# Padded queries in the first attention, modulation steps moved, small loads issued earlier

## The chip, the cores and the metric

The kernel runs on one core of a Trainium2 chip. The metric is the device time of one execution in microseconds (us). The engines, each with its own instruction row that runs in order: TensorE (PE; its weight loads are a row of their own, PEld), VectorE (DVE), ScalarE (ACT), GpSimd (POOL) and SyncE (SP). SP, ACT and POOL also issue the DMA transfers.

## The reference, cut to what matters

Two transformer blocks, batch 1, 256 tokens, width 1024. The change touches the first, which has two layers: differential attention with a gated FFN, then a pooling mixer with a gated FFN. Both layers are modulated by vectors made from `c`.

```python
def adaln_params(cond, w_mod, b_mod):
    m = jax.nn.silu(cond) @ w_mod + b_mod
    return jnp.split(m, N_MOD, axis=-1)

def diff_softmax_mix(q, k, v, lam):
    s = jnp.einsum('bqhmd,bkhmd->bhmqk', q * (HEAD_DIM ** -0.5), k).astype(jnp.float32)
    p = jax.nn.softmax(s, axis=-1)
    a = p[:, :, 0] - lam * p[:, :, 1]
    return jnp.einsum('bhqk,bkhe->bqhe', a.astype(v.dtype), v)

def first_block(...):
    for i in range(DEPTH):                      # 2 layers
        sh1, sc1, g1, sh2, sc2, g2 = adaln_params(c[:, None, :], w_mod[i], b_mod[i])
        hx = h * (1 + sc1) + sh1                # and the same for the context in layer 0
        # layer 0: 8 heads, each with two maps m = 0, 1 of 64 columns; 256 queries, 512 keys
        # layer 1: multi-scale pooling
        x = layer_norm(ALPHA * x + g1 * y_lat, ln_g[i, 0], ln_b[i, 0])
        x = layer_norm(ALPHA * x + g2 * swiglu(modulate(x, sh2, sc2), ffn_w_in[i], ffn_w_out[i]), ln_g[i, 1], ln_b[i, 1])
```

## The kernel before, in words

**Products.** Products of weights and activations are made in three passes (`mm3`, L77 to L80): both operands are split in a high and a low part, and high x high, high x low and low x high are added up in PSUM. A weight block (1 MB) is loaded by SP into one of four `raw` buffers (`raw_load`, L51), and `wsplit` (L57) makes `whi` (an ACT cast, L70) and `wlo` (a DVE subtraction, L71), each in two halves.

**Order.** The program is written in the Tile framework. Its scheduler sets the order of instructions of each engine when the program is built, by its own planning; `behind(...)` keeps an instruction from being issued before another. After that each engine runs its row in order. A DMA of SP or ACT signals its end in one of eight places, taken in turn by both engines' loads; a new load waits for the load that had its place before (`DMAHW0` to `DMAHW7` in the order below).

**Loading.** The loop `for q in range(4)` (L621) loads a quarter of the first two modulation vectors' weights (two raws), a quarter of `x` and of the context, and the rows of the attention's weights for it. `mod_quarter` makes the modulation, `modulate` transposes and modulates the inputs (`hf`, L567), `fill` splits the attention's weights, and `products` and `rest` make the projections of group 0. After the loop seven small loads are issued by ACT behind the last `hf`: five into `prow` (norm gains and biases; transposed by PE at L648 to `pcol`), `rope` (the tables of the rotary embedding) and `lamr`.

**Attention.** Four groups of two heads (L755). `rope_T` rotates the keys and then the queries and transposes them (L690); `split_to` splits them in high and low. A block of scores (`scores`, L693) is one head and one half of the queries: for each of the two maps a 128 x 512 score tile in a PSUM bank of its own (`sbank`, two buffers), in three passes, each over the 64 rows of that map (L706). Then two reductions on DVE (L708), two exps on ACT (L710), and the mix of the maps (L713), which is transposed (L717). There are 16 blocks.

**The modulation stream.** `mod_stream` (L198) makes ten further modulation vectors in ten groups of eight steps; a step is a 512 KB load by POOL into one of three `mraw` buffers (L131) and a multiply and add on DVE (L132). Steps are strewn by `mod_step` over attention (2 behind each score block), the first FFN's first product (3 at a time) and its second product (1 behind each of 11 units). A group ends in `acc_col` (L138) or `acc_row` (L145) on PE. The ninth group is `g1_1`, whose last step is the 72nd.

**The second FFN product** (`Ffn.out`, L452): 11 units of 24 products with 512 columns, of which the last two units' 48 are held for `finish`. Those stand `behind(mods["mm"])` (L846), that is, behind the last L145 of `g1_1`.

## Time and profile before

| | |
|---|---|
| median of 3 runs | 1158.36 us (1158.08 to 1160.95) |
| profiled execution | 1157.81 us, its span 1156.0 us |
| PE busy / PEld busy | 98% / 90% of the span |
| DVE / ACT / POOL busy | 72% / 50% / 7% |
| DMA | 229.69 MB, mean 199 GB/s |
| loading and first modulation | 0 to 72 us |
| attention, 16 score blocks | 72 to 210 us |
| first FFN, first product | 250 to 374 us |
| first FFN, second product | 375 to 439 us |

The stages are read from the trace by the first and last instructions of their lines. A busy share is a mean over stages; where one engine is busy all the time, the others' idle time costs nothing there. Busy time of PE counts an overlap of two matmuls once; the duration of one matmul (the second number of a row of the timeline) is longer than the step to the next one's start, since they are pipelined.

### The profile page before, as it was taken

To read this page: it belongs to the slowest core of one execution; us is meant where nothing else is said; L and a number is where in the kernel's file an instruction comes from. 1 tells how busy PE (TensorE), PEld (TensorE's weight loads), DVE (VectorE), ACT (ScalarE), POOL (GpSimd) and SP (SyncE) were. 2 spreads that over 40 slices of the span, in tenths; PEclk is the share of its full clock that TensorE was granted. 3 is DMA by queue.
4 is the path that set the end of the run, shared out by engine and by line. 5 is a ranking of instruction groups with operands and counts; after the bars stand their busy time and mean duration, and the time that the engine had idled before them with its cause. 6 is when DMAs were issued, how large, how long until landed. Compare 5 with 4: busy or idle time off the path is not lost. (4 is left out here: it accounts for less than half of the span.)

```text
span 1156.0 us, 19870 instructions
## 1 busy us (share of the span) xinstructions
PE 1129.1 (98%) x7967; PEld 1035.3 (90%) x7967; DVE 829.0 (72%) x1547; ACT 575.8 (50%) x1017; POOL 83.9 (7%) x154
## 2 busy tenths in 40 slices
PE   8989999999999999999999889999999999999998
PEld 7979988889999877999988779989999989999986
DVE  5677887887887877856654779788788674655541
ACT  5643444576444436654543655455346356545430
POOL 0101110100111111000000020000100000000000
PEclk9999999999999999999999999999999999999999
DMA  9956545648998993867565353660456254664530
GB/s 311 324 174 212 183 155 174 219 146 285 313 317 291 341 353 121 249 217 257 210 222 175 109 180 121 179 200 29 146 160 223 77 178 147 219 199 167 215 113 37
DMA packets 149098, 229.69 MB, mean 199 GB/s; under 512 B 5708, under 2 KB 121051, under 8 KB 149006
## 3 DMA queue, kind: packets, MB, share of 16 engines
q1 hardware_dynamic: 133440, 176.10, 46.6%
q0 software_dynamic: 14672, 50.63, 13.0%
q10 hardware_dynamic: 894, 1.69, 0.5%
q8 instruction: 63, 1.03, 0.4%
q14 instruction: 29, 0.24, 0.1%
HBM read 226.36 MB, written 2.04 MB: 198 GB/s over the span
## 5 line engine op out<-in xcount | busy, mean ns | idle before, releaser
L71 DVE TENSOR_TENSOR wlo<-raw,whi 128x1024 fp32r<-128x1024 f32 (+2 forms) x318 | 372.7, 1193 | 135.2 <-ACT whi L70 133.7
L70 ACT CAST whi<-raw 128x1024 fp32r<-128x1024 f32 (+2 forms) x318 | 316.3, 1028 | 229.6 <-PE mm L80 86.7
L78 PE MATMUL mm<-hTh,whi 128*128 128x256 f32 x1056 | 299.1, 283 | 0.0
L80 PE MATMUL mm<-hTh,wlo 128*128 128x256 f32 x1056 | 298.9, 283 | 0.0
L79 PE MATMUL mm<-hTl,whi 128*128 128x256 f32 x1056 | 298.3, 282 | 0.0
L79 PEld LDWEIGHTS mm<-hTl,whi 128*128 128x128 f32 x1056 | 199.4, 189 | 0.3
L78 PEld LDWEIGHTS mm<-hTh,whi 128*128 128x128 f32 x1056 | 199.3, 189 | 0.3
L80 PEld LDWEIGHTS mm<-hTh,wlo 128*128 128x128 f32 x1056 | 199.3, 189 | 0.1
L78 PE MATMUL mm<-whi,hTh 128*128 128x256 f32 (+4 forms) x592 | 185.5, 314 | 2.3 <-DVE hTh L336 1.8
L80 PE MATMUL mm<-whi,hTl 128*128 128x256 f32 (+4 forms) x592 | 184.8, 313 | 0.4 <-DVE hTl L337 0.4
L79 PE MATMUL mm<-wlo,hTh 128*128 128x256 f32 (+4 forms) x592 | 184.3, 312 | 0.6 <-DVE wlo L71 0.6
L78 PEld LDWEIGHTS mm<-whi,hTh 128*128 128x128 f32 x592 | 112.4, 190 | 9.0 <-DVE hTh L336 2.9
L79 PEld LDWEIGHTS mm<-wlo,hTh 128*128 128x128 f32 x592 | 112.3, 190 | 4.9 <-DVE wlo L71 1.0
L80 PEld LDWEIGHTS mm<-whi,hTl 128*128 128x128 f32 x592 | 111.9, 189 | 5.2 <-DVE hTl L337 1.0
L132 DVE SCALAR_TENSOR_TENSOR acc<-mraw,csil,acc 128x1024 f32<-128x1024 f32 x80 | 102.2, 1280 | 10.0 <-DMA mraw<-in_w_mod_dram 9.6
L78 PE MATMUL mm<-whi,hid 128*128 128x512 f32 x264 | 104.3, 395 | 0.0
L79 PE MATMUL mm<-wlo,hid 128*128 128x512 f32 x264 | 104.2, 395 | 0.0
L80 PE MATMUL mm<-whi,hid 128*128 128x512 f32 x264 | 103.7, 393 | 0.0
L131 POOL DMA_DIRECT2D mraw<-in_w_mod_dram x80 | 42.6, 533 | 367.8 <-DVE acc L132 269.8
L79 PEld LDWEIGHTS mm<-wlo,hid 128*128 128x128 f32 x264 | 49.6, 188 | 11.6 <-issue 1.0
L80 PEld LDWEIGHTS mm<-whi,hid 128*128 128x128 f32 x264 | 49.6, 188 | 11.5 <-issue 0.7
L78 PEld LDWEIGHTS mm<-whi,hid 128*128 128x128 f32 x264 | 49.6, 188 | 11.4 <-issue 0.7
(329 smaller groups left out, 1556.6 us busy)
## 6 DMA issues: line engine op xcount, KB each, us to landing
raw<-in_ffn_w_in_dram SPq DMA_DIRECT2D x44, 1024.0 KB, 7.1
mraw<-in_w_mod_dram POOLq DMA_DIRECT2D x80, 512.0 KB, 5.0
raw<-in_ffn_w_out_dram SPq DMA_DIRECT2D x22, 1024.0 KB, 4.9
raw<-in_w_ffn_in_dram SPq DMA_DIRECT2D x22, 1024.0 KB, 5.2
raw<-in_w_in_dram SPq DMA_DIRECT2D x16, 1024.0 KB, 5.5
raw<-in_w_ffn_out_dram SPq DMA_DIRECT2D x11, 1024.0 KB, 5.0
raw<-in_w_in_dram SPq DMA_DIRECT2D x14, 768.0 KB, 4.4
raw<-in_attn_w_qkv_dram SPq DMA_DIRECT2D x9, 1024.0 KB, 8.4
```

The lines of the kernel that those rows point to most:

```text
L70: se.copy(hv[:, sl], raw[:, sl])
L71: seq["sub"] = ve.tensor_sub(lv[:, sl], raw[:, sl], hv[:, sl].bitcast(F32)).ins
L78: pe.matmul(o, lh, rh, start=first, stop=False, **kw)
L79: pe.matmul(o, lh, rl, start=False, stop=False, **kw)
L80: return pe.matmul(o, ll, rh, start=False, stop=last, **kw).ins
L131: gp.dma_start(raw, wv[:, k, g * 1024:(g + 1) * 1024])
L132: ve.scalar_tensor_tensor(acc, raw, csil[:, k, 0:1], acc, op0=ALU.mult, op1=ALU.add)
```

## The change

Three things are changed.

1. The queries are kept in a tile `QZ` with 128 rows for each map: the map's own 64 rows hold the query, the other 64 hold zeros, written once by POOL. A score matmul then runs over all 128 rows of the keys and gives the same sums. `split_to` is called once for each map's rows. The passes are written map by map instead of in turns.
2. The small loads into `prow`, `rope` and `lamr` are issued at `q == 1` of the loading loop instead of behind it.
3. The steps of the modulation stream: behind a score block 1 instead of 2; 1 behind the last `rope_T` addition of a group and 2 behind its last mix, so 7 per group instead of 8; in the first FFN's second product 2 at units 2, 4, 6 and 8.

```diff
-STEPS_S, STEPS_IN, STEPS_OUT = 2, 3, 1
+STEPS_S, STEPS_IN, STEPS_OUT = 1, 3, 1
...
             for u in range(11):
                 o.unit(u)
                 with behind(seq["sub"]):
-                    mod_step(mod_out)
+                    mod_step(mod_out * (2 if u in (2, 4, 6, 8) else 1))
...
             modulate(q)
+            if q == 1:
+                with behind(seq["mod"]):
+                    prow = cp.tile([128, 128], F32, name="prow")
+                    gp.memset(prow, 0.0)
+                    se.dma_start(prow[32:64], I["ln_g"].rearrange("l w (k c) -> (l w k) c", c=128))
+                    se.dma_start(prow[64:96], I["ln_b"].rearrange("l w (k c) -> (l w k) c", c=128))
+                    se.dma_start(prow[96:104], rows128(I["norm1_g_2"][0]))
+                    se.dma_start(prow[104:112], rows128(I["norm2_g_2"][0]))
+                    se.dma_start(prow[112:113], I["attn_subln_g"])
+                    rope = at.tile([128, 2, 2, 2, 64], F32, name="rope")
+                    se.dma_start(rope, I["k_rope"].rearrange("(t p) v w c -> p t v w c", p=128))
+                    lamr = at.tile([128, 256], F32, tag="aT", name="lamr", bufs=5)
+                    se.dma_start(lamr, I["attn_lambda"].rearrange("a b c -> a (b c)").to_broadcast([128, 256]))
...
-            ve.tensor_add(r12[:, 0, :], r12[:, 0, :], r12[:, 1, :])
+            seq["rope"] = ve.tensor_add(r12[:, 0, :], r12[:, 0, :], r12[:, 1, :]).ins
...
+        QZ = [at.tile([128, 2, 2, 256], F32R, name=f"QZ{i}") for i in range(2)]
+        for a in QZ:
+            for m in range(2):
+                gp.memset(a[(1 - m) * 64:(2 - m) * 64, m].bitcast(F32), 0.0)
...
-            last = ()
-            for i, (q, k) in enumerate(((qh, kh), (qh, kl), (ql, kh))):
-                for m in range(2):
-                    p = slice(m * 64, (m + 1) * 64)
-                    with behind(*last):
-                        last = pe.matmul(Sm[m], q[p, h, tk], k[p, h, :], start=i == 0, stop=i == 2).ins,
+            for m in range(2):
+                for i, (q, k) in enumerate(((QZ[0], kh), (QZ[1], kh), (QZ[0], kl))):
+                    pe.matmul(Sm[m], q[:, m, h, tk], k[:, h, :], start=i == 0, stop=i == 2)
...
-            rope_T(cq.PL, *[lat(a) for a in qhl], 1)
+            qT = rope_T(cq.PL, 1)
+            for m in range(2):
+                p = slice(m * 64, (m + 1) * 64)
+                split_to(*[lat(a[p, m]) for a in QZ], qT[p])
+            with behind(seq["rope"]):
+                mod_step()
...
+            with behind(seq["mix"]):
+                mod_step(2)
             head_out(aTs, vt, g, sm)
```

SP in the loading, before: from the attention's weight rows of the third quarter (`raw`, 128x2x256) to the modulation weights of the fourth (`raw`, 128x8x256) and its `x`. In brackets stands what an instruction waits for.

```order
L526 DMA raw<-in_attn_w_qkv_dram 128x2x256 [waits DMAHW7_49,DVE_49]
L526 DMA raw<-in_attn_w_qkv_dram 128x2x256 [waits DMAHW0_49]
L498 DMA xin<-in_ctx_dram 128x256 [waits DMAHW1_49]
L498 DMA xin<-in_ctx_dram 128x256 [waits DMAHW2_49]
L526 DMA raw<-in_attn_w_qkv_dram 128x2x256 [waits DMAHW3_49]
L54 DMA raw<-in_w_mod_dram 128x8x256 [waits DMAHW4_49,DVE_49]
L54 DMA raw<-in_w_mod_dram 128x8x256 [waits DMAHW5_49,DVE_49]
L495 DMA x<-in_x_dram 128x2x256 [waits DMAHW6_49]
```

SP, the same loads after:

```order
L526 DMA raw<-in_attn_w_qkv_dram 128x2x256 [waits DMAHW0_49,DVE_49]
L526 DMA raw<-in_attn_w_qkv_dram 128x2x256 [waits DMAHW3_49]
L498 DMA xin<-in_ctx_dram 128x256 [waits DMAHW5_49]
L498 DMA xin<-in_ctx_dram 128x256 [waits DMAHW7_49]
L526 DMA raw<-in_attn_w_qkv_dram 128x2x256 [waits DMAHW1_49]
L54 DMA raw<-in_w_mod_dram 128x8x256 [waits DMAHW3_49,DVE_49]
L54 DMA raw<-in_w_mod_dram 128x8x256 [waits DMAHW4_49,DVE_49]
L495 DMA x<-in_x_dram 128x2x256 [waits DMAHW5_49]
```

The loads are the same and in the same order; the places whose earlier loads they wait for are others, because ACT's seven loads now take places in between.

ACT in the same part, before: the `hf` activations of the second quarter, and the casts of the third quarter's modulation weights (`whi`, L70, and `we`, L514) and attention weights (`whi`, L588).

```order
L70 CAST whi<-raw 128x1024 [waits DMAHW4_49,Activation_49]
L567 ACTIVATE hf<-tp,modc 128x256 [waits PE_49]
L567 ACTIVATE hf<-tp,modc 128x256
L70 CAST whi<-raw 128x1024
L514 CAST we<-raw 128x1024 [waits DMAHW5_49,Activation_49]
L514 CAST we<-raw 128x1024 [waits Activation_49]
L588 CAST whi<-raw 128x512 [waits DMAHW7_49]
```

ACT after; L636 to L644 are the seven small loads:

```order
L567 ACTIVATE hf<-tp,modc 128x256 [waits PE_49]
L567 ACTIVATE hf<-tp,modc 128x256
L636 DMA prow<-in_ln_g_dram 32x128 [waits Pool_49]
L637 DMA prow<-in_ln_b_dram 32x128 [waits DMAHW1_49]
L638 DMA prow<-in_norm_g_dram 8x128 [waits DMAHW2_49]
L639 DMA prow<-in_norm_g_dram 8x128
L640 DMA prow<-in_attn_subln_g_dram 1x128 [waits DMAHW6_49]
L642 DMA rope<-in_k_rope_dram 128x2x256 [waits DMAHW0_49]
L644 DMA lamr<-in_attn_lambda_dram 128x256 [waits DMAHW2_49]
L70 CAST whi<-raw 128x1024
L514 CAST we<-raw 128x1024 [waits DMAHW5_49,Activation_49]
L588 CAST whi<-raw 128x512
```

The small loads moved from behind the fourth quarter's last `hf` to the place between the second quarter's `hf` and the second half of the third quarter's first cast.

PE in group 0 of attention, before: part of the second score block (`s<-k,q`, L706) among projections (L78 to L80).

```order
L80 MATMUL mm<-whi,hTl 128x256
L706 MATMUL s<-k_741,q_739 128x512
L78 MATMUL mm<-whi,hTh 128x256
L79 MATMUL mm<-wlo,hTh 128x256
L80 MATMUL mm<-whi,hTl 128x256
L706 MATMUL s<-k_741,q_739 128x512
L706 MATMUL s<-k_742,q_739 128x512 x2
L706 MATMUL s<-k_741,q_740 128x512 x2
L78 MATMUL mm<-whi,hTh 128x256
L79 MATMUL mm<-wlo,hTh 128x256
```

PE after, the first score block of group 0:

```order
L80 MATMUL mm<-whi,hcTl 128x256
L710 MATMUL s<-k_745,QZ_739 128x512
L710 MATMUL s<-k_745,QZ_740 128x512
L710 MATMUL s<-k_746,QZ_739 128x512
L710 MATMUL s<-k_745,QZ_739 128x512
L710 MATMUL s<-k_745,QZ_740 128x512
L710 MATMUL s<-k_746,QZ_739 128x512
L78 MATMUL mm<-whi,hTh 128x256
L79 MATMUL mm<-wlo,hTh 128x256
L80 MATMUL mm<-whi,hTl 128x256
```

A block was issued in pieces between projections; now its six matmuls with `QZ` stand together or in two threes.

DVE at the end of the first FFN's second product, before: L71 are the splits of the weights of units 8, 9 and 10, and, in the last row, of the next weights; L132 are the steps of the modulation, the last one the 72nd.

```order
L71 TENSOR_TENSOR wlo<-raw,whi 128x1024 [waits DMAHW7_49,Activation_49]
L71 TENSOR_TENSOR wlo<-raw,whi 128x1024 [waits Activation_49]
L132 SCALAR_TENSOR_TENSOR acc<-mraw,csil,acc 128x1024 [waits DMASW6_49,DVE_49]
L71 TENSOR_TENSOR wlo<-raw,whi 128x1024 [waits DMAHW0_49,Activation_49]
L71 TENSOR_TENSOR wlo<-raw,whi 128x1024 [waits Activation_49]
L132 SCALAR_TENSOR_TENSOR acc<-mraw,csil,acc 128x1024 [waits DMASW7_49,DVE_49]
L71 TENSOR_TENSOR wlo<-raw,whi 128x1024 [waits DMAHW1_49,Activation_49]
L71 TENSOR_TENSOR wlo<-raw,whi 128x1024 [waits Activation_49]
L132 SCALAR_TENSOR_TENSOR acc<-mraw,csil,acc 128x1024 [waits DMASW0_49,DVE_49]
L132 SCALAR_TENSOR_TENSOR acc<-mraw,csil,acc 128x1024 [waits DMASW1_49,DVE_49]
L132 SCALAR_TENSOR_TENSOR acc<-mraw,csil,acc 128x1024 [waits DMASW2_49,DVE_49]
L71 TENSOR_TENSOR wlo<-raw,whi 128x1024 [waits DMAHW3_49,Activation_49]
```

DVE after, the splits of units 9 and 10 (the first two pairs of L71), the steps behind unit 8 from the third on, and the next weights' split (the last two L71):

```order
L71 TENSOR_TENSOR wlo<-raw,whi 128x1024 [waits DMAHW0_49,Activation_49]
L71 TENSOR_TENSOR wlo<-raw,whi 128x1024 [waits Activation_49]
L132 SCALAR_TENSOR_TENSOR acc<-mraw,csil,acc 128x1024 [waits DMASW4_49,DVE_49]
L132 SCALAR_TENSOR_TENSOR acc<-mraw,csil,acc 128x1024 [waits DMASW5_49,DVE_49]
L132 SCALAR_TENSOR_TENSOR acc<-mraw,csil,acc 128x1024 [waits DMASW6_49,DVE_49]
L71 TENSOR_TENSOR wlo<-raw,whi 128x1024 [waits DMAHW1_49,Activation_49]
L71 TENSOR_TENSOR wlo<-raw,whi 128x1024 [waits Activation_49]
L132 SCALAR_TENSOR_TENSOR acc<-mraw,csil,acc 128x1024 [waits DMASW7_49,DVE_49]
L132 SCALAR_TENSOR_TENSOR acc<-mraw,csil,acc 128x1024 [waits DMASW0_49,DVE_49]
L71 TENSOR_TENSOR wlo<-raw,whi 128x1024 [waits DMAHW3_49,Activation_49]
L132 SCALAR_TENSOR_TENSOR acc<-mraw,csil,acc 128x1024 [waits DMASW1_49,DVE_49]
L71 TENSOR_TENSOR wlo<-raw,whi 128x1024 [waits Activation_49]
```

Behind the split of unit 8 there are nine steps up to the 72nd, where there were five; the 72nd (its row is the next behind those shown) also has two halves of the next weights' splits ahead of it.

## Rows read from the trace of the kernel before

**Rows 1.** Stretches: busy us of PE, PEld, DVE, ACT, POOL; PEclk; DMA share; GB/s.

```profile
10.00:40.00 30.00, 28.89 (x238) 24.68 (x236) 22.72 (x35) 20.69 (x31) 0.00 (x0) 1.00 1.09 348
66.00:70.00 4.00, 4.00 (x23) 4.00 (x24) 4.00 (x9) 1.53 (x2) 0.00 (x0) 0.61 0.01 4
400.00:420.00 20.00, 20.00 (x90) 16.59 (x89) 17.51 (x15) 7.33 (x8) 3.75 (x8) 1.00 1.00 349
676.00:680.00 4.00, 4.00 (x25) 3.42 (x24) 3.75 (x13) 2.20 (x9) 0.00 (x0) 1.00 0.56 124
```

**Rows 2.** Timeline, PE, second score block: start us, us, instruction.

```profile
75.47 0.28 PE L80 MATMUL mm<-whi,hTl 128*128 128x256 f32 x1
75.68 0.50 PE L706 MATMUL s<-k,q 64*128 64x512 f32 x1
76.11 0.39 PE L78 MATMUL mm<-whi,hTh 128*128 128x256 f32 x1
...
76.45 0.28 PE L80 MATMUL mm<-whi,hTl 128*128 128x256 f32 x1
76.66 0.96 PE L706 MATMUL s<-k,q 64*128 64x512 f32 x5
77.55 0.38 PE L78 MATMUL mm<-whi,hTh 128*128 128x256 f32 x1
```

**Rows 3.** Groups of instructions, 72 to 240: busy us, mean ns of one | idle before.

```profile
L706 PE MATMUL s<-k,q 64*128 64x512 f32 x96 | 22.4, 447 | 0.3
```

**Rows 4.** Timeline, PE, second product of the first FFN.

```profile
400.67 0.39 PE L78 MATMUL mm<-whi,hid 128*128 128x512 f32 x1
...
402.48 0.39 PE L80 MATMUL mm<-whi,hid 128*128 128x512 f32 x1
```

**Rows 5.** Groups of instructions, DVE, 72 to 238: split of the queries.

```profile
L674 DVE TENSOR_TENSOR q<-tp,q 128x512 fp32r<-128x512 f32 x4 | 2.8, 692 | 3.5 <-ACT q L673 3.5
```

**Rows 6.** Waits, 50 to 72 us: total, times, longest (DVE, PE).

```profile
DVE pcol L650 <- PE s L648: 4.5, 1, 4.5
DVE r L684 <- DMA rope<-in_k_rope_dram: 1.6, 1, 1.6
...
PE s L648 <- DMA prow<-in_norm_g_dram: 0.7, 1, 0.7
```

**Rows 7.** Timeline, PE, around the first rotated transposes [idle before <-releaser].

```profile
63.12 0.28 PE L80 MATMUL mm<-whi,hcTl 128*128 128x256 f32 x1
65.94 0.65 PE L690 MATMUL tp<-idsel,r 128*128 128x128 f32 x4 [2.55 <-DVE r L687]
```

**Rows 8.** Timeline, ACT's issues: the first and the last of seven.

```profile
53.21 0.32 ACTq L642 DMA_DIRECT2D prow<-in_ln_g_dram  x1
...
55.73 0.48 ACTq L658 DMA_DIRECT2D lamr<-in_attn_lambda_dram  x1
```

**Rows 9.** Timelines, ACT and SP, in the loading.

```profile
31.19 1.05 ACT L70 CAST whi<-raw 128x1024 fp32r<-128x1024 f32 x1
...
28.73 5.42 SPq L54 DMA_DIRECT2D raw<-in_w_mod_dram  x2
```

**Rows 10.** SP's waits; DMA issues (KB each, us to landing), 0 to 72.

```profile
SPq L54 <- DMA prow<-in_ln_g_dram: 8.2, 1, 8.2
...
prow<-in_ln_g_dram ACTq DMA_DIRECT2D x1, 16.0 KB, 2.9
```

**Rows 11.** Timelines, DVE and PE, at the end of group g1_1.

```profile
420.13 1.28 DVE L132 SCALAR_TENSOR_TENSOR acc<-mraw,csil,acc 128x1024 f32<-128x1024 f32 x1 [0.79 <-DMA mraw<-in_w_mod_dram]
424.49 1.28 DVE L132 SCALAR_TENSOR_TENSOR acc<-mraw,csil,acc 128x1024 f32<-128x1024 f32 x1 [3.07 <-DMA mraw<-in_w_mod_dram]
...
425.31 0.39 PE L80 MATMUL mm<-whi,hid 128*128 128x512 f32 x1
425.87 1.96 PE L145 MATMUL s<-acc,ones 128*128 128x512 f32 x4 [0.17 <-issue]
```

**Rows 12.** Timeline, PE, start of the second block.

```profile
675.73 0.30 PE L956 MATMUL tp<-idsel,pr 128*128 128x128 f32 x1 [3.15 <-DMA pr<-in_qk_norm_g_dram]
```

More of the change, by code (lines that the diff above doesn't have):

```diff
@@ L654, in tile_net @@
             N1, N2 = pcol[:, 96:104], pcol[:, 104:112]
-            rope = at.tile([128, 2, 2, 2, 64], F32, name="rope")
-            se.dma_start(rope, I["k_rope"].rearrange("(t p) v w c -> p t v w c", p=128))
-            lamr = at.tile([128, 256], F32, tag="aT", name="lamr", bufs=5)
-            se.dma_start(lamr, I["attn_lambda"].rearrange("a b c -> a (b c)").to_broadcast([128, 256]))
             lsum = at.tile([128, 4], F32, name="lsum")
@@ L760, in tile_net @@
                 cq.products(ALLK)
[L761 removed]
             khl = [at.tile([128, 2, 512], F32R, tag=f"k{i}", name=f"k{i}", bufs=1) for i in range(2)]
             lat = lambda a: a.rearrange("p h (t c) -> p t h c", t=2)
[L764 removed]
+            split_to(*[lat(a[:, :, 256:512]) for a in khl], rope_T(ck.PL, 0))
             split_to(khl[0][:, :, 0:256], khl[1][:, :, 0:256], ck.PC)
[L766 removed]
+            qT = rope_T(cq.PL, 1)
[4 more added lines that the diff above has]
+                mod_step()
             if not g:
@@ L773, in tile_net @@
                 for h in range(2):
-                    aTs[t, h] = scores(*qhl, *khl, h, t, sm[:, 2 * t + h, :])
+                    aTs[t, h] = scores(*khl, h, t, sm[:, 2 * t + h, :])
                     with behind(seq["mix"]):
```

15 lines of the change are left out of this document (3 added, 12 removed).

## The prediction

> **What bounds the kernel now.** I read the share of busy time per engine first, then stretches of the span, then what TensorE (PE) does at the places the diff touches. In the stretches [rows 1] the reader should see that PE is busy 28.89 of 30 us while the first weights load and 20.00 of 20 us near the end of the first FFN, and that the DMA engines are full in both (share 1.09 and 1.00, 348 and 349 GB/s). So time is won only where PE idles, waits, runs at the lower clock or spends long on few products, and what delays PE costs its full length. Three places count: the start up to 72 us, the 16 score blocks (72 to 210 us), and the second product of the first FFN (375 to 439 us). Outside them the order of work is the same apart from a few shifts.
>
> The sum is made against the profiled execution, 1157.8 us; the median of the runs is 1158.4, so 0.6 is added at the end. A measurement of this kernel can tell about 0.3% (3.5 us) from no change.
>
> **Part 1, scores on 128 rows.** Now a block has six 64-row matmuls of 512 columns, in pairs on opposite halves of the rows. The two of a pair run together: 96 of 447 ns would be 42.9 us, and the line's busy time is 22.4 [rows 3]. But a block is mostly split in two, with a projection matmul between, and each turn from 128-row to 64-row work and back costs extra [rows 2]: from the L80 at 75.47 to the L78 at 76.11 are 0.64 us, where the pitch of these 256-column lines is 0.12 (half of the 0.226 below), so a lone score matmul costs 0.52; the other five, 76.45 to 77.55, cost 1.10 - 0.12 = 0.98. Together 1.50 per block; 12 of the 16 blocks are split so, the other four (six matmuls in one piece) take 1.35 by the same reading. After the change a block is six full-row matmuls of 512 columns. Their price stands in the FFN: eight steps from 400.67 to 402.48 [rows 4], 0.226 each, 1.36 per block. Gain: 12 x 0.14, less 4 x 0.01, about 1.7 us.
>
> Against it: the padded query needs its split in two calls per half of the rows, one VectorE (DVE) subtraction more per group (0.69 us [rows 5]), and one ScalarE (ACT) cast more; the order puts fewer projections between the blocks (13 to 16 instead of 21 to 32), and DVE's chain per block (two reductions, reciprocal, mix, one step of the modulation at 1.28) is about as long as PE's spacing then. The trace shows no such spacing; I take 0.25 us of new waiting per group, 1 us in all, between nothing and 4.8 (0.3 per block). **Part 1: -0.7 us, between -1.7 and +3.1.** The four memsets are on GpSimd (POOL) ahead of any use, the fewer DVE steps (7 for 8 per group) beside PE's work: nothing.
>
> The Trainium skill speaks against this part: "TensorE: Matmul & The Clock Gate", Part 3 on packing small matmuls, says that matmuls on different row groups run at the same time, a few ns apart, and that a lone matmul with few rows takes as long as a full one. The pairs of this trace do start together, so the rule holds for them. By it alone a block would cost 3 x 0.226 = 0.68 now and 1.36 after, a loss of 11 us over 16 blocks; the measured 1.50 of a block, turns included, is why I don't sum by it.
>
> **Part 2, small loads moved up.** What they cost now, at 53 to 70 us: ACT issues the seven loads from 53.21 to 56.21 [rows 8]; PE waits 0.7 us for prow; DVE sits 4.5 us behind the transposed prow and 1.6 for the rope table [rows 6], so the rotated keys are late and PE idles 2.55 us before L690 at 65.94 [rows 7]. Behind that idle time PE's granted clock falls to the 1.2 GHz level: its mean in 66 to 70 is 0.61 [rows 1], which is 0.39 x 4 = 1.6 us of work lost. All of it can go: 0.7 + 2.55 + 1.6 = 4.8 us. It is the whole gain only if nothing is late next.
>
> What is late next: the same seven issues, 3.0 us, now stand in ACT's row in the loading, behind the second quarter's `hf`, ahead of the second half of a weight cast that ran at 31.19 [rows 9]; rope and lamr also wait there for earlier loads of their ring place. Behind that cast on ACT are all casts of the third quarter, and PE's products of it. ACT's idle times later in this quarter are waits for these same products and absorb nothing. On SyncE (SP), the ring of eight completion places is shared: seven are taken by ACT's loads, so that SP's context loads and the first modulation weights of the fourth quarter stand behind them. Before, SP issued those at 28.73 [rows 9]. That such a wait is real the trace shows where the loads now lie: SP sat 8.2 us on a weight load until prow landed, and a prow load takes 2.9 us [rows 10]. From 31.2 (ACT's place) + 0.3 + 2.9 = 34.4: up to 5.7 us late on a queue which keeps the DMA engines full. PE has 1.1 us of idle time in these 30. I take the ACT cost, 3.0 us, between 0 (hidden by products of the quarter before) and 5.7; the likely value is nearer the ACT rows than the SP one, since the DMA engines have some us of work queued. A new idle time could halve the clock once more (1.6). **Part 2: -4.8 + 3.0 = -1.8 us, between -4.8 and +2.5.**
>
> **Part 3, modulation steps spread.** Each of the 80 steps is a 512 KB load by POOL and a DVE instruction of 1.28 us. Attention has 28 instead of 32; the second FFN product 15 instead of 11 (two at units 2, 4, 6, 8). The step that ends the group g1_1, the 72nd, is the same one, and it is a gate: PE's last 48 products of the FFN stand behind L145, which needs that step. Before, the gate was just met: the last product ahead of it is at 425.31, L145 at 425.87; DVE had waited 0.79 and 3.07 us for the loads of the last two steps, which ran at 420.13 and 424.49 [rows 11]. There is no slack, so each us the 72nd step is later is a us of PE. By the order, DVE has nine steps after the split of unit 8 where it had five, and two halves of a weight split before the last. Lower bound, DVE alone: 4 x 1.2 (pitch) + 2 x 1.2 - (0.79 + 3.07) = 3.3 us. By bytes: 4 x 512 KB = 2.1 MB more to land before the gate while the DMA engines are full, at 349 GB/s [rows 1] 6.0 us. Upper: about 8, if loads of the next layer's weights come between. I take the bytes, since DVE's last two waits there were for loads. PE may then idle long enough to fall to 1.2 GHz (1.6 us again); it did after 2.55 us [rows 7], but not after 3.15 us before 675.73 [rows 12], where the stretch behind has 1.00 [rows 1], so this stays in the range. Fewer steps in attention give PE nothing back, as DVE there is hidden behind PE. **Part 3: +6.0 us, between 0 and +9.6** (0: the loads come through faster than the full engines suggest, and the steps end before PE is there).
>
> Sum: 1157.8 - 0.7 - 1.8 + 6.0 = 1161.3; with 0.6, 1161.9 us.
>
> **Rivals.**
> A, *faster: the steps are hidden and the start gains whole.* The steps come two at a time from unit 2 on, and 3 loads are in flight, so loads may run further ahead of PE than I think; ACT's issues may lie beside PE's products of the quarter before. 1157.8 - 4.8 - 1.7 + 0.6 = 1151.9. Against it: full DMA engines in both places.
> B, *no change: the gate costs DVE's time only.* 1157.8 - 0.7 - 1.8 + 3.3 + 0.6 = 1159.2. It decides by whether the loads of the last steps land before DVE asks.
> C, *slower, by the start: the small loads stop the big ones.* SP behind ACT's loads, 5.7 us, and the lower clock again: part 2 is +2.5, the total 1157.8 - 0.7 + 2.5 + 6.0 + 0.6 = 1166.2. It decides from some 4.8 us of delay in the third quarter, where the gain is eaten.
> D, *the padding does double work.* If a pair costs one pitch and the turns are paid in both kernels, a block goes from 3 x 0.226 to 6 x 0.226, and 16 blocks lose 11 us: 1157.8 + 11 - 1.8 + 6.0 + 0.6 = 1173.6. The rows for 1.50 per block speak against it. This is the rule of the Trainium skill told above.
>
> **How the numbers follow.** My forecast has 0.40, with an own range of 1159 to 1166; of it 0.12 falls within 0.3%. A has 0.27, B 0.16, C 0.13, D 0.04. Faster: A, 0.27. Same: B and that 0.12, 0.28. Slower: 0.28 + 0.13 + 0.04 = 0.45. The range that leaves out no more than 2 in 10 goes from the middle of A to the upper part of C: 1152 to 1168.
>
> **What would show it.** Part 1: score blocks of six matmuls 0.23 apart with no turns, and 1.3 to 1.4 us per block; waits for DVE's reductions or exps beside them tell the price against it. Part 2: no idle time of 2.55 before the first rope transpose and no 0.61 behind it, but the weight cast of the third quarter at 34 instead of 31, and SP's loads for the fourth later than 28.7. First scores earlier than before show a net gain. Part 3: PE idle by 4 to 8 us before L145 of g1_1 with DVE or the mraw loads as releaser. If PE passes that gate with under a microsecond of waiting, my forecast is wrong and A is right; if the start is later than before, C is.

## The result, and the profile after

The changed kernel takes 1174.3 us (median of 4 runs, 1170.6 to 1175.1) where the kernel before takes 1159.2: the ratio is 1.0133, with a 95% interval of 1.0116 to 1.015. It is 15 us slower; 3.5 had been forecast, and the time lies above the stated range of 1152 to 1168. The profiled execution is 1175.1 us, the slowest of its four and 17.3 more than that of before, so the shares below add up to 17.3 and not to 15.

Where the time went can be read by lining the two traces up by work: each matmul of PE is taken at its columns divided by 2.4 GHz, added up over PE's row, and for a point of the trace before I looked when the changed kernel had done as much. The table is worked out so from the traces (us later than the profiled execution of before; negative is earlier); the columns are times of the trace before. 55 lies in the loading, 72 at the first scores, 250 behind attention and its output product, 374 behind the first FFN's first product, 425 just ahead of the gate, 445 behind it. The kernels from e1 on are the experiments below.

```
kernel           55     72    250    374    425    445   1150
after         +11.9   +6.5   +4.6   +5.5   +6.0  +17.1  +17.3
e1_loads_old   +0.8   +1.0   -1.3   -0.5    0.0  +11.7  +12.0
e2_steps_old  +12.3   +7.0   +8.0   +8.1   +8.1   +7.7   +7.6
e3_qz_only      0.0   -0.2   +2.6   +2.6   +2.6   +2.5   +1.7
e4_loads_only  +7.4   +1.6   +1.4   +1.4   +1.4   +2.4   +2.3
e7_no_gate     +9.4   +4.1   +2.2   +3.0   +3.2   +8.4  +10.3
e9_steps_in   +12.7   +7.4   +5.4  +12.2  +12.2  +13.0  +13.5
e10_loads_sp   +1.4   -3.8   -5.6   -4.8   -4.2   +5.8   +5.8
e12_best       +0.1   -5.1   -2.3   -2.3   -2.3   -1.5    0.0
e13_before_sp  +0.1   -5.5   -5.8   -5.8   -5.8   -5.9   -6.1
e16_act_dummy  +3.9   -1.9   -2.1   -2.1   -2.1   -2.4   -2.7
e20_rope2       0.0   -4.7   -5.1   -5.1   -5.1   -5.4   -4.6
```

So the loading lost 11.9 us and got 5.4 of them back by the start of the scores (the idle time and the lower clock of [rows 7] and [rows 1] are gone); attention gained 1.9, of which 1.4 were lost again up to 425; the gate cost 11.1.

**The loading.** Stretches of the changed kernel; columns as in [rows 1]:
```profile
28.00:34.00 6.00, 6.00 (x52) 5.76 (x52) 3.52 (x7) 2.97 (x5) 0.00 (x0) 1.00 0.74 222
34.00:40.00 6.00, 3.62 (x30) 2.38 (x29) 4.56 (x5) 3.98 (x5) 0.00 (x0) 1.00 0.73 210
40.00:45.00 5.00, 1.97 (x17) 1.67 (x15) 0.83 (x2) 1.59 (x3) 0.00 (x0) 1.00 1.08 355
45.00:50.00 5.00, 3.46 (x15) 3.44 (x16) 3.88 (x9) 3.83 (x7) 0.00 (x0) 0.63 1.09 348
50.00:55.00 5.00, 5.00 (x32) 3.83 (x32) 4.93 (x9) 3.13 (x6) 2.11 (x3) 0.68 0.94 291
```

The DMA share, 1.09 in this part before, is 0.74 and 0.73 from 28 to 40; PE is then busy 1.97 of 5 us, and in the ten us behind it the granted clock is 0.63 and 0.68, partly at the 1.2 GHz level, which takes 0.37 x 5 + 0.32 x 5 = 3.4 us of work. Why the DMA engines had nothing to do stands in the timelines of ACT and SP (start us, us, instruction, idle time before it and what ended it), beside [rows 8] and [rows 9]:
```profile
30.39 0.32 ACTq L636 DMA_DIRECT2D prow<-in_ln_g_dram  x1
32.44 0.40 ACTq L642 DMA_DIRECT2D rope<-in_k_rope_dram  x1
33.95 0.37 ACTq L644 DMA_DIRECT2D lamr<-in_attn_lambda_dram  x1
34.36 1.04 ACT L70 CAST whi<-raw 128x1024 fp32r<-128x1024 f32 x1 [2.96 <-DMA prow<-in_norm_g_dram]
...
30.90 2.79 SPq L498 DMA_DIRECT2D xin<-in_ctx_dram  x2
33.74 0.44 SPq L526 DMA_DIRECT2D raw<-in_attn_w_qkv_dram  x1
34.27 2.79 SPq L54 DMA_DIRECT2D raw<-in_w_mod_dram  x2
37.11 3.74 SPq L495 DMA_DIRECT2D x<-in_x_dram  x1
```

SP's waits from 20 to 60 us of the changed kernel that the trace before doesn't have (total, times, longest):
```profile
SPq L498 <- DMA raw<-in_w_mod_dram: 4.3, 1, 4.3
SPq L498 <- DMA prow<-in_ln_g_dram: 2.1, 1, 2.1
```

The cast moved from 31.19 to 34.36, as worked out. SP's modulation weights moved from 28.73 to 34.27. That is the 34.4 of the upper bound, but in part by luck: SP waited 2.1 us for a `prow` load, as the bound has it, and 4.3 us for an earlier load of modulation weights, whose place its context load now has to wait for since ACT's loads took others. Both queues were late, where the prediction took one of them.

**The gate.** PE and DVE of the changed kernel at the end of the group g1_1, beside [rows 11]. The first L145 row closes the group ahead of it (g2_0), the second closes g1_1:
```profile
430.12 0.40 PE L80 MATMUL mm<-whi,hid 128*128 128x512 f32 x1
430.36 1.88 PE L145 MATMUL s<-acc,ones 128*128 128x512 f32 x4
440.26 3.75 PE L145 MATMUL s<-acc,ones 128*128 128x512 f32 x4 [8.03 <-issue]
...
432.10 2.60 DVE L132 SCALAR_TENSOR_TENSOR acc<-mraw,csil,acc 128x1024 f32<-128x1024 f32 x2 [2.62 <-DMA mraw<-in_w_mod_dram]
435.76 1.28 DVE L132 SCALAR_TENSOR_TENSOR acc<-mraw,csil,acc 128x1024 f32<-128x1024 f32 x1
438.87 1.28 DVE L132 SCALAR_TENSOR_TENSOR acc<-mraw,csil,acc 128x1024 f32<-128x1024 f32 x1 [0.70 <-DMA mraw<-in_w_mod_dram]
...
436.00:440.00 4.00, 0.00 (x0) 0.00 (x0) 3.30 (x3) 0.00 (x0) 0.53 (x1) 0.50 0.89 292
440.00:444.00 4.00, 3.74 (x5) 1.71 (x6) 2.43 (x3) 0.58 (x1) 0.53 (x1) 0.50 0.85 250
444.00:448.00 4.00, 4.00 (x16) 3.18 (x15) 1.57 (x2) 0.58 (x1) 1.45 (x2) 0.79 1.07 377
```

The 72nd step, at 424.49 before, runs at 438.87; PE is idle 8.03 us ("issue" names no releaser, but L145 starts as the step ends, 438.87 + 1.28). Behind the idle time the clock is at the lower level up to some way into 444 to 448: 0.5 x 3.7 + 0.21 x 4 = 2.7 us.

**The scores.** A block of the changed kernel on PE, and the group of its score matmuls over 72 to 250 us, beside [rows 2] and [rows 3]:
```profile
83.53 0.28 PE L79 MATMUL mm<-wlo,hTh 128*128 128x256 f32 x1
83.65 0.87 PE L710 MATMUL s<-k,QZ 128*128 128x512 f32 x3
84.36 0.60 PE L721 MATMUL tp<-idsel,e 128*128 128x128 f32 x4
84.72 0.95 PE L710 MATMUL s<-k,QZ 128*128 128x512 f32 x3
85.50 0.28 PE L80 MATMUL mm<-whi,hTl 128*128 128x256 f32 x1
...
L710 PE MATMUL s<-k,QZ 128*128 128x512 f32 x96 | 29.1, 414 | 0.4 <-ACT QZ L676 0.3
```

The turn in front is gone (the first score matmul follows its projection by 0.12 us), but the two threes take 0.71 and 0.78 us to the next instruction, 1.49 for the block. That is what a block took before (1.50); 1.36 had been predicted. A three behind the transposes takes more than 3 x 0.226 = 0.68. Over all 16 blocks the same reading (from the instruction ahead to the one behind, less the pitch of the one ahead) gives 1.49 per block before and 1.62 after, short waits included.

### The profile page after: what moved, and what is told of

Read it like the earlier page. It is cut to its first block, busy times and chain, and to the rows that moved or that the text cites. A ratio compares the mean times of both kernels' runs of the same rounds, so it can differ in the third digit from the quotient of the medians.

```text
span 1173.3 us, 19881 instructions
## 1 busy us (share of the span) xinstructions
PE 1132.3 (97%) x7967; PEld 1043.2 (89%) x7967; DVE 833.6 (71%) x1551; ACT 579.0 (49%) x1021; POOL 86.1 (7%) x158
## 5 line engine op out<-in xcount | busy, mean ns | idle before, releaser
L71 DVE TENSOR_TENSOR wlo<-raw,whi 128x1024 fp32r<-128x1024 f32 (+2 forms) x318 | 373.2, 1193 | 146.1 <-ACT whi L70 145.6
L70 ACT CAST whi<-raw 128x1024 fp32r<-128x1024 f32 (+2 forms) x318 | 316.3, 1027 | 240.4 <-PE mm L80 89.0
L78 PE MATMUL mm<-hTh,whi 128*128 128x256 f32 x1056 | 298.8, 283 | 0.0
L80 PE MATMUL mm<-hTh,wlo 128*128 128x256 f32 x1056 | 298.4, 283 | 0.0
L78 PEld LDWEIGHTS mm<-hTh,whi 128*128 128x128 f32 x1056 | 199.1, 189 | 0.3
L80 PEld LDWEIGHTS mm<-hTh,wlo 128*128 128x128 f32 x1056 | 199.1, 189 | 0.1
L78 PE MATMUL mm<-whi,hTh 128*128 128x256 f32 (+4 forms) x592 | 184.7, 312 | 3.4 <-DVE hTh L336 1.9
L80 PE MATMUL mm<-whi,hTl 128*128 128x256 f32 (+4 forms) x592 | 183.9, 312 | 0.4 <-DVE hTl L337 0.4
L78 PEld LDWEIGHTS mm<-whi,hTh 128*128 128x128 f32 x592 | 112.1, 189 | 9.0 <-DVE hTh L336 2.9
L80 PEld LDWEIGHTS mm<-whi,hTl 128*128 128x128 f32 x592 | 111.7, 189 | 5.1 <-DVE hTl L337 1.3
L132 DVE SCALAR_TENSOR_TENSOR acc<-mraw,csil,acc 128x1024 f32<-128x1024 f32 x80 | 102.1, 1280 | 11.0 <-DMA mraw<-in_w_mod_dram 10.6
L78 PE MATMUL mm<-whi,hid 128*128 128x512 f32 x264 | 105.1, 398 | 0.0
L80 PE MATMUL mm<-whi,hid 128*128 128x512 f32 x264 | 104.2, 395 | 0.0
L78 PEld LDWEIGHTS mm<-whi,hid 128*128 128x128 f32 x264 | 49.8, 189 | 11.6 <-issue 1.0
L80 PEld LDWEIGHTS mm<-whi,hid 128*128 128x128 f32 x264 | 49.8, 189 | 11.2 <-issue 0.2
```

Source lines behind the costliest of these rows:

```text
L70: se.copy(hv[:, sl], raw[:, sl])
L71: seq["sub"] = ve.tensor_sub(lv[:, sl], raw[:, sl], hv[:, sl].bitcast(F32)).ins
L78: pe.matmul(o, lh, rh, start=first, stop=False, **kw)
L80: return pe.matmul(o, ll, rh, start=False, stop=last, **kw).ins
L132: ve.scalar_tensor_tensor(acc, raw, csil[:, k, 0:1], acc, op0=ALU.mult, op1=ALU.add)
```

## Experiments

The theory from the two traces was: 6.7 us net at the start from the small loads' new place (6.5 in the table), a gain of some 1.3 from the scores, and 11 at the gate from the four added steps. The rivals stand with each run. Runs of one batch share their runs of the kernel before (1157.7 to 1158.7 us), and ratios go by these.

**e1: the small loads back behind the loading.**
```diff
-            if q == 1:
-                with behind(seq["mod"]):
-                    prow, rope, lamr: tiles and loads
...
         with behind(seq["mod"]):
+            prow, rope, lamr: tiles and loads, as before
             pcol_ps = sbank()
```


> The changed kernel with its small loads back behind the loading loop (part 2 undone, parts 1 and 3 kept). Theory from the two traces: the moved loads cost 6.7 us net up to the first groups of attention, so this kernel gives 1174.3 - 6.7 = about 1167.6 us, PE has no gap of 4.7 us near 42 us, and the gate at L145 still waits some 8 us. Rival (the start's loss is given back later in attention, where PE waits for DVE anyway): within 2 us of 1174.3.

1169.5 us, ratio 1.0104 (1.008 to 1.0128): 4.8 below the changed kernel, where 6.7 had been expected. The loading is as before (+0.8 at 55), and the gate waits 9.20 us. The loss at the start is not given back later: the two kernels are 5.5 us apart at 72 and 5.3 at 1150. Of the 6.5 us at 72, 1.0 stay without the moved loads. Up to the gate, at 425, this kernel is level with the one before, so parts 1 and 3 together change nothing there.

**e2: the steps as before.**
```diff
-STEPS_S, STEPS_IN, STEPS_OUT = 1, 3, 1
+STEPS_S, STEPS_IN, STEPS_OUT = 2, 3, 1
...
-                    mod_step(mod_out * (2 if u in (2, 4, 6, 8) else 1))
+                    mod_step(mod_out)
...
-            with behind(seq["rope"]):
-                mod_step()
...
-            with behind(seq["mix"]):
-                mod_step(2)
```


> The changed kernel with the modulation steps as before (2 behind each score block, 1 behind each unit of the second FFN product; part 3 undone, parts 1 and 2 kept). Theory: the gate before L145 of g1_1 cost 10.8 us (8.4 waiting, the rest the lower clock behind it), so 1163.5 us, with PE waiting under 1 us at L145. Rival (the gate is late because the start left the loads late, not because of the four more steps): a wait of 5 us or more at L145 stays, 1169 us or more.

1163.5 us, ratio 1.005 (1.0031 to 1.007): 10.8 below, as expected, though the start is as late as in the changed kernel. PE passes the L145 of g1_1 without a wait:
```profile
430.23 1.02 PE L145 MATMUL s<-acc,ones 128*128 128x512 f32 x2
433.60 1.88 PE L145 MATMUL s<-acc,ones 128*128 128x512 f32 x4
```

The gate's wait comes from the steps, not from the late start.

**e3: padded queries alone** (the edits of e1 and e2 together on the changed kernel).

> The kernel before with part 1 alone (padded queries, scores on 128 rows). Theory: the blocks lose their turns between 64-row and 128-row work and gain 1.3 us, 1159.2 - 1.3 = 1157.9 us. Rival (pairs of matmuls on opposite row halves were worth their overlap): slower by 3 to 11 us, 1162 to 1170 us. Second rival (the split's extra call and shorter spacing make DVE late): within 1 us above 1159.2.

1163.0 us, ratio 1.0033 (1.0014 to 1.0051): slower by 3.8 of 1158.2, where a gain of 1.3 was expected. In its trace, of an execution 3.4 us faster than the median, the place of the work is even up to 125 us, 2.1 us are lost by 150 and 2.6 by 250. Its waits of PE, 72 to 250 us (total, times, longest), against none of these two in the trace before:
```profile
PE s L138 <- DVE acc L132: 1.6, 2, 1.2
PE s L145 <- DVE acc L132: 0.7, 1, 0.7
```

It is like the gate: the products that close a vector (`acc_col`, `acc_row`) stand in PE's row and wait for its last step. Besides, the granted clock is 0.89 from 140 to 155 us, 1.6 us of work, where it is 1.00 before. The theory on the scores had to be changed (e15, e12, e20).

**e5: the small loads by POOL**, which takes no place in the ring and no time of ACT.
```diff
-                    se.dma_start(prow[32:64], ...
+                    gp.dma_start(prow[32:64], ...
                     (and so for all seven)
```


> The changed kernel with the seven small loads at the same early place, but issued by POOL, not by ACT: they take no place in the ring that SP and ACT share and no time of ACT. Theory (the ring and ACT's issue time held up SP's weight loads, and the DMA engines ran dry): the loss of 11.4 us in the loading vanishes and the gain of 4.8 us stays, 1174.3 - 11.4 = about 1163 us. Rival (the bytes and small packets of these loads in the full DMA engines cost it): 1172 us or more.

1165.8 us, ratio 1.0073 (1.0052 to 1.0093). The test was not the one intended: `behind` didn't hold POOL back, the loads went out in the first microseconds of the program, ahead of the first weights, and the start lost 5.0 us by 20 us; by 72 all of it was regained. e5c repeats it with the loads held at their place.

**e4: the kernel before with the moved loads alone** (part 2 of the change's diff and nothing else).

> The kernel before with part 2 alone (small loads issued by ACT at the second quarter). Theory (the ring holds SP's loads up, the DMA engines run dry): the net loss of 6.7 us of the changed kernel's start shows here too, 1158.2 + 6.7 = 1165 us, and DMA share under 0.8 in 28 to 40 us. Rival (the loss belongs to the combination with the new order of the attention): within 3.5 us of before.

1162.2 us, ratio 1.0037 (1.0018 to 1.0057), between the two expectations: slower by 4.3, not by 6.7. The loading loses 7.4 us here (11.9 in the changed kernel) at a granted clock of 0.88 and 0.80 in 34 to 45 us, which takes 0.12 x 6 + 0.2 x 5 = 1.7 us against the 3.4 of the changed kernel. The DMA share in 28 to 34 us is 0.75 here and 0.74 there. PE, ACT, DVE and SP run the same instructions in the same order through the whole loading in this kernel, the changed one, e2, e7 and e9, and yet the loss at 55 us is 7.4, 11.9, 12.3, 9.4 and 12.7: one trace tells the price of the loading to some 5 us. The trace here is of the fastest of ten executions (1160.1 to 1168.4). By the medians the moved loads cost 4.5 us in this kernel and 4.8 in the changed one (e1).

**e7: the FFN's last products not behind the gate.**
```diff
-                with behind(mods["mm"]):
-                    n2.pre(t, n, o2.finish(t, n), mods["g2_0"])
+                n2.pre(t, n, o2.finish(t, n), mods["g2_0"])
```


> The changed kernel, but the last 48 products of the first FFN no longer stand behind L145 of g1_1 (the two places where the layer norm's first step was put behind it are freed). Theory (PE waits only because these products are put behind the late step): 1174.3 - 10.8 = 1163.5 us, with no wait of over 2 us in 430 to 445. Rival (the late step holds up DVE and the norm behind it just as long, so the wait moves behind the products): 1170 us or more.

1169.9 us, ratio 1.009 (1.0055 to 1.0124): 4.4 less than the changed kernel, and at the edge of the rival's 1170. The edit did not take the gate out of PE's way: of the 48 products 27 still stand behind the last L145 in PE's row, and PE waits there. DVE's row has the 72nd step ahead of the norm's first instruction (L254):
```profile
437.41 2.38 PE L145 MATMUL s<-acc,ones 128*128 128x512 f32 x4 [2.92 <-issue]
...
436.02 1.28 DVE L132 SCALAR_TENSOR_TENSOR acc<-mraw,csil,acc 128x1024 f32<-128x1024 f32 x1 [0.74 <-DMA mraw<-in_w_mod_dram]
437.22 2.35 DVE L71 TENSOR_TENSOR wlo<-raw,whi 128x1024 fp32r<-128x1024 f32 x2
439.49 0.68 DVE L254 TENSOR_TENSOR z<-mm,acc 128x512 f32<-128x512 f32 x1
```

By lining up by work, 5.2 us are lost between 425 and 445, against 11.1. The 2.92 us of waiting and the lower clock behind it (0.60 from 438 to 442, 1.6 us) make most of them. With 21 products moved ahead of the wait it is shorter by 5.1 us; what the late step would cost without any gate on PE, through DVE's row alone, this run doesn't show.

**e9: the four steps in the FFN's first product instead.**
```diff
-                    mod_step(mod_in)
+                    mod_step(mod_in + (mod_in > 1 and fp in (2, 4, 6, 8)))
...
-                    mod_step(mod_out * (2 if u in (2, 4, 6, 8) else 1))
+                    mod_step(mod_out)
```


> The changed kernel with the four added steps in the first product of the first FFN (one more at its units 2, 4, 6 and 8) instead of the second; the 72nd step has the same number of steps behind unit 8 as before. Theory (four more 512 KB loads where the DMA engines are full make the gate late): the wait at L145 falls under 1 us, 1174.3 - 10.8 = 1163.5 us. Rival (the steps cost as much wherever the FFN's weights are loaded): 1170 us or more.

1171.4 us, ratio 1.0094 (1.0065 to 1.0123): only 3 less. The gate is passed with 0.8 us lost, as the theory has it, but 6.8 us are lost in 250 to 374. PE's waits there:
```profile
PE s L138 <- issue: 2.0, 1, 2.0
PE s L138 <- DVE acc L132: 0.9, 1, 0.9
```

These are products that close vectors of the stream; a granted clock of 0.95 from 350 to 382 takes 1.6 us more, and the rest of the 6.8 is not accounted for. The rival holds: where the FFN's weights stream, four steps cost in either product, though the DMA share of the first product is 0.85 to 0.89 before, not full.

**e10: the small loads on SP behind the fourth quarter's loads.**
```diff
                 raws, rw = load_quarter(q)
+            if q == 3:
+                prow, rope, lamr: tiles and loads, with sp.dma_start
```


> The changed kernel with the seven small loads issued by SP behind the fourth quarter's loads: no time of ACT, and no place in the ring ahead of the loading's weights. Theory (not the bytes, but their place ahead of the weights cost it): start gains all it can, 1174.3 - 11.4 = 1163 us, first rotated transposes without the idle time of 2.5 us. Rival (they then hold up the next group's weights on SP by as much): 1170 us or more.

1162.6 us, ratio 1.0033 (1.0018 to 1.0049): 11.7 below the changed kernel, as expected. PE in the changed place, beside [rows 7]:
```profile
60.05 0.27 PE L653 MATMUL s<-idsel,prow 128*128 128x128 f32 x1
60.16 0.60 PE L690 MATMUL tp<-idsel,r 128*128 128x128 f32 x4
```

No idle time of 2.55 us, and the granted clock in 66 to 72 is 1.00. From 55 to 72 the kernel gains 5.2 us, where part 2 worked out 4.8 for the gain.

**e5c: POOL again, held at the second quarter** by a small POOL instruction that reads that quarter's modulation.
```diff
-                    gp.memset(prow, 0.0)
+                    gp.tensor_scalar(prow, modc[:, 3, 0:1].to_broadcast([128, 128]), 0.0, None, op0=ALU.mult)
...
+                    gp.tensor_copy(rope[:, 0, 0, 0, 0:2], modc[:, 3, :])
+                    gp.tensor_copy(lamr[:, 0:2], modc[:, 3, :])
                     (and the seven loads with gp.dma_start)
```


> The changed kernel with the small loads issued by POOL, held back by a small POOL instruction that reads the second quarter's modulation, so that they start at about the time at which the changed kernel's ACT issues them. Theory (place in the ring and time of ACT, not the transfers): the DMA engines stay full in 28 to 40 us and the start gains: 1174.3 - 11.4 = 1163 us. Rival (the transfers themselves, many small packets in full engines, delay the weights): 1170 us or more.

1164.6 us, ratio 1.006 (1.0038 to 1.0082): 9.7 below the changed kernel. The loads run at 29 to 33 us, ACT's at 30 to 34, and the DMA engines stay full:
```profile
28.00:34.00 6.00, 6.00 (x52) 5.70 (x52) 4.84 (x9) 5.76 (x9) 4.88 (x10) 1.00 1.09 348
34.00:40.00 6.00, 6.00 (x52) 5.18 (x51) 3.79 (x7) 2.17 (x5) 0.00 (x0) 1.00 1.08 344
```

Only 0.8 us are lost at 55. The transfers themselves don't cost the 11.9 us; the queues they were put in do.

**e16: 3 us of ACT time alone**, on the kernel before with the small loads on SP (e13).
```diff
             modulate(q)
+            if q == 1:
+                with behind(seq["mod"]):
+                    junk = at.tile([128, 22, 128], F32, name="junk")
+                    se.copy(junk, ones[:, None, :].to_broadcast([128, 22, 128]))
```


> The kernel before with the small loads on SP behind the loading (1153.4 us) and one copy of 2816 columns (about 2.9 us) put on ACT at the place where the changed kernel's ACT issues the small loads. Theory ring (SP's loads waited for ACT's in the ring, DMA ran dry): 3 us of ACT alone cost under 1.5 us, 1153 to 1155. Theory ACT time (the late casts are the loss): 3 us or more, 1156.5 or more.

1156.0 us, ratio 0.9986 (0.9972 to 1.0001): 2.6 above e13. ACT, SP and the stretch of the loading:
```profile
31.48 2.56 ACT L646 COPY junk<-ones 128x2816 f32<-128x2816 f32 x1
33.92 1.05 ACT L70 CAST whi<-raw 128x1024 fp32r<-128x1024 f32 x1
...
28.74 7.89 SPq L54 DMA_DIRECT2D raw<-in_w_mod_dram  x2
...
28.00:34.00 6.00, 6.00 (x51) 5.74 (x52) 3.51 (x7) 5.39 (x7) 0.00 (x0) 1.00 1.09 348
34.00:40.00 6.00, 4.44 (x36) 2.88 (x34) 4.99 (x6) 4.42 (x7) 0.00 (x0) 1.00 0.79 252
```

The cast at 33.92, 2.7 us late, costs as much: the theory of ACT's time holds for 2.6 to 3.8 us (the table has 3.9 at 55 against e13's 0.1), and from 34 on here too the DMA engines lose their work, since the raw buffers come free later, though SP issues its first load at 28.74 as before. From 28 to 34 us the share is 1.09 here and 0.74 in the changed kernel, whose cast is only 0.4 us later: that part is SP's. The rest of the 11.9 us, some 8, is put down to the ring and the lower clock by subtraction; no run holds SP back and leaves ACT alone. The two were not rivals; both cost.

**e18: the loads of g1_1 left out**, on e10.
```diff
         for k in range(8):
+            if (layer, g) == (1, 2):
+                ve.scalar_tensor_tensor(acc, acc, csil[:, k, 0:1], acc, op0=ALU.mult, op1=ALU.add)
+                yield acc
+                continue
```


> The changed kernel with the small loads on SP (1162.6 us, gate's wait some 8 us). Left out: the loads of the ninth group g1_1; its eight steps compute on the accumulator itself, DVE's instructions and their number stay. Theory bytes (the loads of the last steps land late): the wait at L145 falls under 1 us, about 1153 us. Theory DVE (nine steps and two split halves are too long by themselves): a wait of 3 us or more stays, 1156 or more.

1154.8 us, ratio 0.9971 (0.9958 to 0.9983). The last two L145 groups (L149 in this kernel), and e10's second one below:
```profile
418.79 1.88 PE L149 MATMUL s<-acc,ones 128*128 128x512 f32 x4
422.04 1.96 PE L149 MATMUL s<-acc,ones 128*128 128x512 f32 x4 [1.37 <-ACT acc L150]
...
429.68 3.75 PE L145 MATMUL s<-acc,ones 128*128 128x512 f32 x4 [7.72 <-issue]
```

With all of DVE's instructions in place the wait is 1.37 us instead of 7.72. The loads make the gate late; DVE's own time is 1.4 of it, less than the 3.3 I had as the lower bound. All eight loads of the group are gone here, 4.2 MB and not only the four added ones, so the run says that the loads decide, not what four of them cost.

**e15: padded queries with eight steps per group, spread in attention;** second FFN product and small loads as before.
```diff
-            with behind(seq["mix"]):
-                mod_step(2)
+            with behind(seq["mix"]):
+                mod_step(3)
```


> The kernel before with padded queries and the modulation steps of attention spread, but all eight per group kept there (1 behind the last rotation, 1 behind each block, 3 behind the last mix) and the second FFN product as before; small loads at the old place. Theory (two steps behind each block made DVE late for the closer full-row blocks; one step fits): scores gain 1.3 us, 1158 - 1.3 = 1156.7 us, where the padded queries alone gave 1163.0. Rival (full-row blocks are slower by themselves): 1162 us or more.

1161.4 us, ratio 1.0038 (1.0018 to 1.0058): slower than before, the theory of two steps behind each block is not enough. The closing products don't wait in its trace (0.11 us at most). PE waits 2.5 us for the heads' outputs ahead of their transposes, 0.4 before, and the granted clock is 0.66 from 100 to 105 us, 1.7 us of work, just behind a closing.

**e13: the kernel before with the small loads on SP behind the loading** (e10's edit on the kernel before).

> The kernel before with the small loads issued by SP behind the fourth quarter's loads and nothing else. Theory: the idle time of 2.5 us and the lower clock behind it vanish and the loading is not disturbed: 1158 - 4.8 = 1153.2 us. Rival (the gain needs the padded queries' order): within 2 us of before.

1153.4 us, ratio 0.996 (0.9943 to 0.9977): the expected gain (5.1 below the median of before, 4.8 worked out), and faster than both kernels.

**e12: e15 with the small loads on SP.**

> Padded queries, eight steps per group spread over attention, second FFN product as before, small loads on SP behind the loading. Theory (the gains add, and neither the ring nor the gate is touched): 1158 - 4.8 - 1.3 = 1152 us. Rival (a later stage is full and takes it back, as the first FFN's first product did with four more steps): 1156 us or more.

1157.6 us, ratio 0.9998 (0.9982 to 1.0014): 4.2 above e13, which has no padded queries. The first difference in attention arises at 128 us; PE's row and DVE's:
```profile
129.57 1.61 PE L138 MATMUL s<-ones,acc 128*128 128x1 f32 x13 [1.29 <-DVE acc L132]
...
128.23 1.28 DVE L132 SCALAR_TENSOR_TENSOR acc<-mraw,csil,acc 128x1024 f32<-128x1024 f32 x1 [1.47 <-DMA mraw<-in_w_mod_dram]
```

Again a closing product waits for a step, and the step for its load. Behind it the granted clock is 0.89 from 125 to 140 us, 1.6 us of work; in e13 and e20 it is 1.00 there. The wait and the clock together are the 2.8 us by which e12 is behind e20 at 250.

**e20: the eighth step at the rotation instead of behind the last mix,** otherwise e12.
```diff
             with behind(seq["rope"]):
-                mod_step()
+                mod_step(2)
...
-                mod_step(3)
+                mod_step(2)
```


> Padded queries, small loads on SP, second FFN product as before, eight steps per group of attention: 2 behind the last rotation, 1 behind each block, 2 behind the last mix. Theory place (a step at the group's end is late for the products that close a vector on PE): no wait over 1 us before L138, 1152 us. Theory number (DVE has room for seven only): 1156 us or more, as with the eighth behind the last mix.

1153.3 us, ratio 0.9958 (0.9944 to 0.9972). No closing product waits over 1 us: the place was it, not the number. With padding, e20 is as fast as e13 without it (1153.3 and 1153.4), but the two differ in the places of the steps too, so this doesn't give the worth of padding alone.

**e17 and e19: the four steps behind the units of the product with attn_w_o,** small loads on SP; e17 with padded queries, e19 without.
```diff
             o1.unit(u)
+            with behind(seq["sub"]):
+                mod_step()
```


> Padded queries, seven steps per group in attention, the four left steps behind the four units of the product with attn_w_o, second FFN product as before, small loads on SP behind the loading. Theory (these steps lie where the DMA engines have room, share 0.5 to 0.8, so nothing waits): 1158 - 4.8 - 1.3 = 1152 us. Rival (four steps cost wherever they are put, as in the first FFN product): 1156 us or more.

> As the kernel with four steps at attn_w_o and small loads on SP, but without the padded queries (scores on 64 rows in pairs, as before). Theory (padding gains 1.3 us by the end of the turns): 1153.4 us, 1.3 above its padded twin. Rival (padding costs by DVE's extra split): 1 us or more below its padded twin.

1166.8 us (ratio 1.0076, 1.0048 to 1.0104) and 1170.2 us (1.0106, 1.0081 to 1.0131): a miss. Between 230 and 250 us both lose some 17 us. PE and DVE of e17:
```profile
229.44 3.49 PE L138 MATMUL s<-ones,acc 128*128 128x1 f32 x16 [3.71 <-DVE acc L132]
...
222.42 1.28 DVE L132 SCALAR_TENSOR_TENSOR acc<-mraw,csil,acc 128x1024 f32<-128x1024 f32 x1 [3.25 <-DMA mraw<-in_w_mod_dram]
```

A closing stands on PE behind the output product's first units, with the last head's transposes and the norm behind it; its wait of 3.71 us is followed by a granted clock of 0.50 and 0.52 from 230 to 240. A mean DMA share of 0.5 to 0.8 did not mean room for a step on time. The pair is the one with equal steps and padding alone between them: padded, it is ahead by 1.0 us at 220 and by 3.4 in the median. The other such pair, e3 against the kernel before, has padding 3.8 us behind. So the worth of padding depends on where the steps stand.

## Why the prediction was wrong

**The direction and the places were right, two terms too small.** Lined up by work the terms are: part 1, with the steps of part 3 up to the gate, 0.0 (e1 at 425; predicted -0.7), part 2 +6.0 (the changed kernel against e1 at 425; 4.8 in the medians; predicted -1.8), the gate of part 3 +11.1 (10.8 in the medians, e2; predicted +6.0), and +0.2 behind.

**Part 2 is the step that failed.** Its gain was right: 5.2 us from 55 to 72 in e10, 5.1 in the median of e13 (predicted 4.8). The cost was taken as 3.0, the time of ACT's issues, with SP's 5.7 us as the other end of a range, "between 0 and 5.7". Both were there at once: e16 has 2.6 us (3.8 in its trace) for ACT's time alone, and the changed kernel's SP is 5.5 us late. SP's lateness was set aside with the reason that the DMA engines have some us of work queued; the share of 0.74 in 28 to 34 us, where e16 has 1.09, shows that they ran dry. On top of that came the lower clock, 3.4 us against the 1.6 in the range, behind a longer idle time of PE (1.97 us busy of the 5 from 40 to 45). The largest loss that the prediction allowed, 5.7 + 1.6, is 7.3; it was 11.9 in this trace and some 9.6 by the medians (the net 4.8 and the gain of 4.8). The two costs and the clock, 3.0 + 5.7 + 3.4 = 12.1, come close to the 11.9, so rival C should have had the sum; that they add up rests on this one trace.

**Part 3 had the right mechanism and cause.** That the gate was just met, that the loads and not DVE decide, and that each us is PE's: e2 (no wait with the old steps) and e18 (1.37 us without the loads). Its size was the bytes alone, 6.0; it measured 8.0 us of waiting and 2.7 of the lower clock, together some 11. The upper end of 8 us was for loads of the next layer's weights in between, and the waiting came to it; that these loads are the 2 us above the bytes was not tested. With the clock, put at 1.6, the range ended at 9.6 and was short by 1.5.

**Part 1 came out near its value by luck.** The turns do go, but a block doesn't get shorter: 1.49 us in the block shown and 1.62 over all, not 1.36. The attention's gain of 1.9 us goes mostly with 28 steps instead of 32: one vector less is closed there (the fourth closes in the first FFN), and its 16 products with one column take PE 1.7 us and count for almost nothing in columns. It is moved, not won: from 250 to 425 us the changed kernel, e1 and e10, with 28 steps, lose 1.3 or 1.4 us, and the kernels with 32 lose 0.1 at most. "The fewer DVE steps beside PE's work: nothing" missed that steps carry closing products with them. e3 and e12 show the other side: with eight steps per group and padding, some 4 us were lost, most of it by closings that waited and by a lower clock behind, and e20 has them back with one step in another place. e15 lost some 3 us without such a wait. What padding alone is worth stays open (e3, and e17 against e19). Of the Trainium skill's rule on row groups ("TensorE: Matmul & The Clock Gate", Part 3): the pairs of before do overlap (their two starts are 3 to 11 ns apart), yet the loss of 11 us that the rule alone gives didn't come (e20 with padding is as fast as e13). The measured block decided. In the 12 split blocks, besides, only two pairs start together and two of the six matmuls run alone, which the 3 x 0.226 of a block before leaves out.

**The rivals.** A's condition at the gate failed (8.0 us of waiting), B's too (DVE alone leaves 1.37). C named the cause at the start with too low a price. D is refuted by the measured blocks, 1.49 and 1.62 us where it has 0.68 and 1.36, and by e20. What stays open: how the 11.9 us of the loading divide between ACT, SP and the clock, and why single executions of the same loading lose between 7.4 and 12.7 us.

The version that beats both kernels is the kernel before with the small loads on SP behind the loading (e13, 1153.4 us), or with padding and the eighth step at the rotation (e20, 1153.3 us).

## What to carry to other kernels

A small load is not free because it is small: look at what stands behind it on the engine that issues it, and at which later loads wait for its completion place; put it at the end of a queue that has slack, here SP behind the last big load, rather than early in a full one. A background stream has to be judged by its deadlines: find each product that needs the last step of a group, and count the loads, not DVE's instructions, between there and the place from which steps are added; a step moved to where the weights stream cost PE time in each place that was tried here. When two queues can each be late, take their sum as the upper bound unless the trace shows that one hides in the other.

## What the runs showed of the hardware

The same seven transfers at about the same time left the DMA engines at a share of 1.09 and 1.08 from 28 to 40 us when POOL issued them (e5c) and at 0.74 and 0.73 when ACT did. The granted clock didn't follow the length of an idle time alone: it stayed at 1.00 behind 3.15 us of idle time [rows 12], fell behind 2.55 us [rows 7], stood at 0.50 behind the 8 us of the gate, and was 0.66 from 100 to 105 us in e15 behind a closing that had waited 0.11. And single executions of one kernel here differ by up to 10 us (e12: 1155.4 to 1165.1; e3: 1157.8 to 1166.5), so the profiled execution of e3 (1159.6) alone would have told of a far smaller loss than its median.
